# Attention scores of a hybrid decoder layer: one product over two key blocks in place of two

## Chip, core and metric

The kernel runs on one core of a Trainium2 chip. The metric is device time in microseconds (us): the median of three runs of the kernel before is 1100.19 us (1099.69 to 1100.69). The engines are named as the profile names them: PE (TensorE) with its weight loads PEld, DVE (VectorE), ACT (ScalarE), POOL (GpSimd) and SP (SyncE, which issues most DMAs).

## What is computed

One decoder layer over 1024 tokens of width 1024, in float32: an input projection, half of whose columns go to sliding-window attention with 8 query heads and 2 key heads of 64, the other half to a gated linear recurrence with four heads of 128; an output projection; and a squared-ReLU MLP of width 4096. What the change touches is the attention, in blocks of 128 queries, each against its own block of keys and the block ahead of it:

```python
def band(a):
    ab = a.reshape(B, nb, WINDOW, ATT_KV_HEADS, D)
    prev = jnp.pad(ab, ((0, 0), (1, 0), (0, 0), (0, 0), (0, 0)))[:, :-1]
    return jnp.concatenate([prev, ab], axis=2)

kk, vv = band(k), band(v)
s = jnp.einsum('bnqhgd,bnkhd->bnhgqk', qb, kk).astype(jnp.float32) * (D ** -0.5)
...
p = p / (jnp.sum(p, axis=-1, keepdims=True) + jnp.exp(sink - m))
o = jnp.einsum('bnhgqk,bnkhd->bnqhgd', p.astype(v.dtype), vv)
```

Here WINDOW is 128, so that there are 8 blocks, and D is 64.

## The kernel before, in words

The layer runs in stages on the one core: the modulation vectors and the first projections, attention (from about 84 to 188 us of the span), the recurrence heads, the output projection, and the MLP, which takes the last 600 us. Most products are split by hand into three float32r products of high and low parts (`proj3`); the attention works on plain float32, for which a product shows as two PE records, two passes.

`attention(tb)` (L523) is a generator for one block of 128 tokens, with two `yield`s inside. Its first part transposes the queries and keys of the block by PE (`pqT`, `pkT`), copies them out (`qT` by ACT, `kT` by DVE, L532 to L534) and forms the scores (L542 to L550): for two pairs of query columns (`mp`), two columns (`m`), the key block ahead and the own one (`src`), and two key heads (`g`) one product of 128 queries by 128 keys each. The key heads lie on partitions 0 to 63 and 64 to 127, so that the two products of a pair use different rows of the array. A block has 16 products, the first block 8. For each `mp`, `g` the scores of the key block ahead are copied out by ACT, and those of the own block go by a masked DVE copy into `comb` (L551 to L555). Maximum, exponentials with their sums (`sm`), the reciprocal `rd` and the scaling of `comb` follow (half on DVE, half on POOL). The second part, after the first `yield`, transposes the weights (`pT`), splits them by the mask into `pc` and `pp`, forms the output `oT`, its squares (`sqa`, ACT), their sum `sqr` (DVE), a transpose of that sum on PE (`ssp`), its sum `ssc`, two POOL operations (`t_att`, `r_att`) and a diagonal `dg`. The third part is one product `rb` (L611) with that diagonal and the scaling of the output (`q<-q,rb`).

The loop at L673 to L679 starts the parts of the 8 blocks against a row of fillers: the projections `pq`, `pk` of blocks 4 to 7, then eight `pv` products (`values`, 24 products of 512 columns each), one filler a step. Within that loop no engine's order is pinned (L640 takes the pins off): the framework's scheduler sets each engine's order from the dependences and its own estimate of times, and on the chip every engine then runs its list in that fixed order. So a filler product can stand between two steps of a block, and a changed instruction can move others. Buffers matter in two places: PSUM tiles of pool `pb` (five banks) hold `pqT`, `pkT`, the scores, `pT` and `oT`; `kT` has three buffers of 128 columns.

Of the kernel before, what the change touches and what calls it, by code (L numbers as in the profile page):

```python
# [9 lines left out]
F32 = mybir.dt.float32  # L10
F32R = mybir.dt.float32r
I32 = mybir.dt.int32
AF = mybir.ActivationFunctionType
# [3 lines left out]
P = 128  # L17
D = 1024
KB = D // P
TB = 8  # L20
# [27 lines left out]
def hybrid_layer(ctx: ExitStack, tc: tile.TileContext, I, out, dbg=None):  # L48
    nc = tc.nc
    ACT, DVE, POOL, PE, SP = (Queue(tc, e) for e in (nc.scalar, nc.vector, nc.gpsimd, nc.tensor, nc.sync))  # L50
# [35 lines left out]
    def t_(name, shape=(P, 512), dt=F32):  # L86
        return T2.tile(list(shape), dt, tag="t2", name=name)
# [4 lines left out]
    def tp_ps(name):  # L92
        return pb.tile([P, 512], F32, tag="b", name=name)
# [166 lines left out]
    XA = gactx.enter_context(tc.tile_pool(name="poolXA", bufs=1))  # L260
# [5 lines left out]
    for gate in range(2):  # L266
        gs = slice(64 * gate, 64 * gate + 64)
# [253 lines left out]
    kTs, vs = {}, {}  # L521

    def attention(tb):  # L523
# [4 lines left out]
        qT = t_(f"qT{tb}", [P, 4, P])  # L528
        ACT.activation(qT, pqT.rearrange("p (m t) -> p m t", m=4), AF.Copy)
        pkT = tp_ps(f"pkT{tb}")  # L530
        PE.transpose(pkT[:, :P], kv[:, 0:P], ident)
        kT = XA.tile([P, P], F32, tag="kT", bufs=3, name=f"kT{tb}")  # L532
        DVE.tensor_copy(kT, pkT[:, :P])
        kTs[tb] = kT  # L534
        aw = q
        a3 = aw.rearrange("p (m t) -> p m t", m=4)
        c5 = w_(f"comb{tb}", (P, 2, 2, 2, P))
# [4 lines left out]
        for mp in range(2):  # L542
            scs = [tp_ps(f"sc{tb}_{mp}_{g}").rearrange("p (m j) -> p m j", m=2) for g in range(2)]
            for m in range(2):
                for src in (tb - 1, tb) if tb else (tb,):
                    for g in range(2):
                        gs = slice(64 * g, 64 * g + 64)
                        js = slice(P, 2 * P) if src == tb else slice(0, P)
                        PE.matmul(scs[g][:, m, js], lhsT=qT[gs, 2 * mp + m, :], rhs=kTs[src][gs, :],
                                  start=True, stop=True)  # L550
            for g in range(2):  # L551
                sc = scs[g]
                if tb:
                    ACT.activation(c5[:, mp, g], sc[:, :, 0:P], AF.Copy)
                DVE.copy_predicated(c5[:, mp, g], mb, sc[:, :, P:2 * P])  # L555
# [33 lines left out]
        for g in range(2):  # L589
            vsl = slice(128 + 64 * g, 192 + 64 * g)  # L590
            og = o_ps[64 * g:64 * g + 64, :].rearrange("p (a x) -> p a x", a=2)
            if tb:
                PE.matmul(og, lhsT=kvn[tb - 1][:, vsl],
                          rhs=pp[:, :, 2 * g:2 * g + 2, :].rearrange("p a m q -> p a (m q)"), start=True, stop=False)
            PE.matmul(og, lhsT=kv[:, vsl], rhs=pc[:, :, 2 * g:2 * g + 2, :].rearrange("p a m q -> p a (m q)"),
                      start=(tb == 0), stop=True)
# [19 lines left out]
    def step(tb):  # L616
        if 0 <= tb < TB:
            next(att[tb])

    att = [attention(tb) for tb in range(TB)]  # L620
    for kb in range(2):
        qproj(kb)
# [962 lines left out]
    g = len(GROUPS) - 1  # L1585
# [3 lines left out]
    for step, (_, t, k) in enumerate(order):  # L1589
# [13 lines left out]
        if k >= 3 and t < 3:  # L1603
            tb = t + 4 * th
# [139 lines left out]
```

## Time and profile before

| what | value |
|---|---|
| median of three runs | 1100.19 us (1099.69 to 1100.69) |
| span of the profiled execution (first to last instruction) | 1097.6 us |
| time of that execution beside its span | not listed; the median lies 2.59 us above the span |
| PE busy | 1076.2 us, 98% of the span |
| DVE, ACT, POOL busy | 795.1, 584.6 and 373.2 us |
| chain that ended last | PE 92%, DVE 3%, ACT 1%, DMA 1%, POOL 1%, issue 1% |
| score products | 240 records, for 120 products |

A PE record of this profile begins where the product begins, but its end is modelled and lies after the beginning of the next one, so the time that a product takes from its engine is the distance from its start to the next start. A number in square brackets at a row's end is idle time of the engine ahead of it and who ended it; a record that is stretched while PE waits can hide such a wait.

### The profile page before, as it was taken

How to read it: one execution, taken by the hardware profiler on the slowest of the kernel's cores; microseconds unless marked ns; L12 is line 12 of the kernel's file. 1: busy time of each engine (PE TensorE's matmuls, PEld its weight loads, DVE VectorE, ACT ScalarE, POOL GpSimd, SP SyncE). 2: the span in 40 equal slices, each digit the busy share in tenths (PEclk: the TensorE clock that was granted, in tenths of full speed). 3: DMA queues.
4: the chain of work that ended last, by engine and by line, in shares of the span. 5: the costliest groups of instructions: out<-in, count | busy, mean ns of one | idle time of the engine just before them, and what ended most of it. 6: DMA issues, size and time to landing. Idle time of an engine off the chain costs nothing.

```text
span 1097.6 us, 16208 instructions
## 1 busy us (share of the span) xinstructions
PE 1076.2 (98%) x5547; PEld 878.2 (80%) x5547; DVE 795.1 (72%) x1323; ACT 584.6 (53%) x1206; POOL 373.2 (34%) x499
## 2 busy tenths in 40 slices
PE   8999999999999999999999999999999999999995
PEld 6788776778888888888888888888888888888884
DVE  4365777878865574559776767876767787899876
ACT  3445544364565764566655555556664543555434
POOL 1153211033324663432543444533333333310014
PEclk9999999999999999999999999999999999999998
DMA  9701301534310352324577676767998888998537
GB/s 347 265 7 57 117 1 43 181 101 140 125 56 11 108 182 96 125 79 144 194 246 249 233 259 227 257 216 244 320 364 289 275 299 259 337 308 272 169 76 131
DMA packets 101587, 203.37 MB, mean 185 GB/s; under 512 B 13025, under 2 KB 13681, under 8 KB 101505
## 3 DMA queue, kind: packets, MB, share of 16 engines
q1 hardware_dynamic: 85968, 154.52, 41.4%
q0 software_dynamic: 15392, 47.57, 14.3%
q8 instruction: 43, 0.70, 0.3%
q14 instruction: 40, 0.32, 0.1%
q10 hardware_dynamic: 144, 0.26, 0.1%
HBM read 147.25 MB, written 55.05 MB: 184 GB/s over the span
## 4 chain that ended last, share of the span: by engine, by line
PE 92%; DVE 3%; ACT 1%; DMA 1%; POOL 1%; issue 1%; SPq 0%; DVEq 0%; POOLq 0%; ACTq 0%
PE pda L39 16%; PE pua L39 14%; PE pdc L39 8%; PE po L39 8%; PE puc L39 7%; PE pu L39 4%; PE pdb L39 4%; PE pq L39 4%; PE phg L39 4%; PE phq L39 3%; PE pub L39 3%; PE phf L39 3%; PE pv L39 3%; PE pk L39 2%; PE o L39 1%; PE sc L39 1%
## 5 line engine op out<-in xcount | busy, mean ns | idle before, releaser
L39 POOL TENSOR_TENSOR b<-b,b 128x512 f32<-128x512 f32 x64 | 89.6, 1400 | 222.8 <-DMA b<-w_dn 222.4
L39 ACT ACTIVATE dw<-dwr 128x512 fp32r<-128x512 f32 x72 | 45.4, 630 | 46.5 <-DMA dwr<-td 32.4
L39 ACT ACTIVATE s<-s 128x512 f32<-128x512 f32 x84 | 53.0, 631 | 31.8 <-DVE s L39 30.5
L39 DVE TENSOR_TENSOR dw<-dwr,dw 128x512 fp32r<-128x512 f32 x72 | 53.6, 744 | 9.0 <-ACT dw L39 8.9
L39 DVE TENSOR_TENSOR acc<-pda,acc 128x512 f32<-128x512 f32 x68 | 46.5, 684 | 13.7 <-PE pda L39 13.3
L39 POOL DMA_DIRECT2D td<-b x64 | 36.3, 567 | 21.6 <-POOL b L39 18.7
L39 POOL TENSOR_TENSOR rrf<-ssf,mhalf 128x1 f32<-128x1 f32 x7 | 7.9, 1253 | 95.3 <-DVE ssf L39 95.3
L39 DVE TENSOR_TENSOR wt<-s,wt 128x512 fp32r<-128x512 f32 x42 | 37.2, 886 | 2.6 <-ACT wt L39 2.5
L39 ACT ACTIVATE s<-pua 128x512 f32<-128x512 f32 x28 | 16.7, 598 | 39.4 <-PE pua L39 33.9
L39 ACT ACT_TABLE_LOAD x28 | 35.9, 1283 | 1.2 <-PEq L1737 0.7
L39 DVE SCALAR_TENSOR_TENSOR macc<-wada,cs,macc 128x512 f32<-128x512 f32 x42 | 33.7, 803 | 3.4 <-DMA wada<-wada 2.9
L39 POOL DMA_DIRECT2D b<-w_dn x64 | 34.4, 540 | 0.0
L39 POOL TENSOR_TENSOR comb<-comb,rd 128x512 f32<-128x512 f32 x8 | 11.7, 1458 | 63.3 <-DVE rd L39 44.2
L39 PE MATMUL pua<-bt_0h,wt 128*128 128x512 f32 x84 | 32.7, 389 | 0.0
L39 PE MATMUL pua<-bt_1h,wt 128*128 128x512 f32 x84 | 32.7, 389 | 0.0
L39 PE MATMUL pua<-bt_3h,wt 128*128 128x512 f32 x84 | 32.7, 389 | 0.0
L39 PE MATMUL pua<-bt_2h,wt 128*128 128x512 f32 x84 | 32.7, 389 | 0.0
L39 DVE TENSOR_TENSOR wt<-a,wt 128x512 fp32r<-128x512 f32 x42 | 31.0, 738 | 0.9 <-ACT wt L39 0.9
L39 DVE TENSOR_TENSOR acc<-pdc,acc 128x512 f32<-128x512 f32 x36 | 24.6, 684 | 8.5 <-PE pdc L39 8.4
L39 ACT ACTIVATE wt<-s 128x512 fp32r<-128x512 f32 x42 | 26.3, 626 | 8.2 <-DVE s L39 8.0
L39 PE MATMUL pda<-dw,du_6h 128*128 128x512 f32 x96 | 29.6, 389 | 0.0
L39 PE MATMUL pda<-dw,du_7h 128*128 128x512 f32 x96 | 29.5, 389 | 0.0
(757 smaller groups left out, 3746.1 us busy)
## 6 DMA issues: line engine op xcount, KB each, us to landing
dur<-ud SPq DMA_DIRECT2D x112, 256.0 KB, 4.5
wada<-wada SPq DMA_DIRECT2D x64, 256.0 KB, 3.5
b<-w_dn POOLq DMA_DIRECT2D x64, 256.0 KB, 5.2
td<-b POOLq DMA_DIRECT2D x64, 256.0 KB, 3.3
dwr<-td SPq DMA_DIRECT2D x64, 256.0 KB, 4.3
a<-w_u SPq DMA_DIRECT2D x56, 256.0 KB, 4.4
dwr<-w_dn SPq DMA_DIRECT2D x48, 256.0 KB, 4.5
ud<-s SPq DMA_DIRECT2D x42, 256.0 KB, 3.6
```

The lines of the kernel that those rows point to most:

```text
L39: ins = op(*args, **kw)
```

## The change

The keys of a block and of the block ahead are put side by side in one tile of 2 x 128 columns. The transposed keys of block `tb` are copied out twice: by DVE into the second half of the block's own tile, and by ACT into the first half of the tile of block `tb + 1`. The scores of a (`mp`, `m`, `g`) are then one product of 256 columns, except in the first block, which has no keys ahead of it. The tile has two buffers in place of three.

```diff
         PE.transpose(pkT[:, :P], kv[:, 0:P], ident)
-        kT = XA.tile([P, P], F32, tag="kT", bufs=3, name=f"kT{tb}")
-        DVE.tensor_copy(kT, pkT[:, :P])
-        kTs[tb] = kT
+        if not tb:
+            kTs[0] = XA.tile([P, 2, P], F32, tag="kT", bufs=2, name="kT0")
+        kT = kTs[tb]
+        DVE.tensor_copy(kT[:, 1], pkT[:, :P])
+        if tb + 1 < TB:
+            kTs[tb + 1] = XA.tile([P, 2, P], F32, tag="kT", bufs=2, name=f"kT{tb + 1}")
+            ACT.activation(kTs[tb + 1][:, 0], pkT[:, :P], AF.Copy)
...
             for m in range(2):
-                for src in (tb - 1, tb) if tb else (tb,):
-                    for g in range(2):
-                        gs = slice(64 * g, 64 * g + 64)
-                        js = slice(P, 2 * P) if src == tb else slice(0, P)
-                        PE.matmul(scs[g][:, m, js], lhsT=qT[gs, 2 * mp + m, :], rhs=kTs[src][gs, :],
-                                  start=True, stop=True)
+                for g in range(2):
+                    gs, js = slice(64 * g, 64 * g + 64), slice(0 if tb else P, 2 * P)
+                    PE.matmul(scs[g][:, m, js], lhsT=qT[gs, 2 * mp + m, :],
+                              rhs=kT.rearrange("p a j -> p (a j)")[gs, js], start=True, stop=True)
```

The scheduler answers with another order. Three places show it. The first is PE in the score part of block 4 (blocks are counted from 0; the tiles' last numbers are buffer numbers). Before, the products with the keys of the block ahead (tile `kT_1460`) stand first, and then two `pv` products and `ssp` (of block 2):

```order
L39 MATMUL sc_0_0_1599<-kT_1460,qT_1592 128x128
L39 MATMUL sc_0_1_1600<-kT_1460,qT_1592 128x128
L39 MATMUL sc_1_0_1613<-kT_1460,qT_1592 128x128
L39 MATMUL sc_1_1_1614<-kT_1460,qT_1592 128x128
L39 MATMUL pv_1831<-whv4l,hhi_0_606 128x512
L39 MATMUL ssp_1577<-c_tab,sqr_1575 128x128
L39 MATMUL pv_1831<-whv4h,hlo_0_607 128x512
L39 MATMUL sc_0_0_1599<-kT_1596,qT_1592 128x128
L39 MATMUL sc_0_1_1600<-kT_1596,qT_1592 128x128
```

Ten more score products and `rb` follow there. Now:

```order
L39 MATMUL sc_0_0_1581<-kT_1449,qT_1573 128x256
L39 MATMUL sc_0_1_1582<-kT_1449,qT_1573 128x256
L39 MATMUL sc_0_0_1581<-kT_1449,qT_1573 128x256
L39 MATMUL sc_0_1_1582<-kT_1449,qT_1573 128x256
L39 MATMUL ssp_1558<-c_tab,sqr_1556 128x128
L39 MATMUL sc_1_0_1591<-kT_1449,qT_1573 128x256
L39 MATMUL sc_1_1_1592<-kT_1449,qT_1573 128x256
L39 MATMUL sc_1_0_1591<-kT_1449,qT_1573 128x256
L39 MATMUL sc_1_1_1592<-kT_1449,qT_1573 128x256
L39 MATMUL rb_1701<-dg_1566,ones 128x128
```

The two `pv` products are gone from the score part, and four score products in place of twelve stand between `ssp` and `rb`. Blocks 4 to 7 have this form in both kernels. Between the last `pT` of a block and the next `oT` there are 20 `pv` products, where the block of the rows below had 21; between `pkT` and the scores there are five, where it had three.

The second place is DVE from the end of the exponentials of block 3 to `ssc` of block 2 and the masked copies of block 4. Before:

```order
L39 TENSOR_TENSOR den_1510<-sm_1501,es_1499 128x8
L39 RECIPROCAL rd_1512<-den_1510 128x8
L39 TENSOR_TENSOR comb_1462<-comb_1462,rd_1512 128x512
L39 TENSOR_TENSOR q_864<-oT_1567,c_attw 128x512
L39 TENSOR_REDUCE sqr_1575<-sqa_1572 128x128
L39 COPY kT_1596<-pkT_1594 128x128
L39 TENSOR_REDUCE ssc_1579<-ssp_1577 128x1
L39 TENSOR_SCALAR dg_1585<-c_tab,r_att_1583 128x128
```

Now:

```order
L39 TENSOR_TENSOR den_1491<-sm_1482,es_1480 128x8
L39 COPY kT_1449<-pkT_1575 128x128
L39 RECIPROCAL rd_1493<-den_1491 128x8
L39 TENSOR_TENSOR q_864<-oT_1548,c_attw 128x512
L39 TENSOR_TENSOR comb_1451<-comb_1451,rd_1493 128x512
L39 TENSOR_REDUCE sqr_1556<-sqa_1553 128x128
L39 COPY_PREDICATED comb_1580<-c_mle,sc_0_0_1581 128x256
L39 TENSOR_REDUCE ssc_1560<-ssp_1558 128x1
L39 COPY_PREDICATED comb_1580<-c_mle,sc_0_1_1582 128x256
L39 TENSOR_SCALAR dg_1566<-c_tab,r_att_1564 128x128
```

The copy of the keys has moved from behind `sqr` to ahead of `rd`; the scaling of `comb` has moved behind `q<-oT`.

The third place is the SP queue behind the attention, where the modulation weights `wada_0_*` and the raw weights of the next head (`whf1r`, `whq1r`) are loaded. Before:

```order
L39 DMA whf1r_2602<-w_hd 128x512
L39 DMA wada_0_0_2370<-wada 128x512
L39 DMA wada_0_1_2373<-wada 128x512
L39 DMA wada_0_2_2376<-wada 128x512
L39 DMA wada_0_3_2379<-wada 128x512
L39 DMA wada_0_4_2382<-wada 128x512
L39 DMA whf1r_2606<-w_hd 128x512
L39 DMA wada_0_5_2385<-wada 128x512
```

Now:

```order
L39 DMA whf1r_2553<-w_hd 128x512
L39 DMA whf1r_2557<-w_hd 128x512
L39 DMA wada_0_0_2321<-wada 128x512
L39 DMA wada_0_1_2324<-wada 128x512
L39 DMA wada_0_2_2327<-wada 128x512
L39 DMA wada_0_3_2330<-wada 128x512
L39 DMA wada_0_4_2333<-wada 128x512
L39 DMA whq1r_2593<-w_hd 128x512
```

One load of a next head's weights has moved ahead of five modulation loads, and the next such load ahead of the other three.

## Rows read from the trace of the kernel before

**Rows 1.** The page: the chain that ended last, by engine.
```profile
PE 92%; DVE 3%; ACT 1%; DMA 1%; POOL 1%; issue 1%; SPq 0%; DVEq 0%; POOLq 0%; ACTq 0%
```

**Rows 2.** PE's timeline: start us, us, instruction, count [idle before <-releaser]. One attention period.
```profile
134.91 0.49 PE L39 MATMUL rb<-dg,ones 128*128 128x128 f32 x2
...
147.44 0.49 PE L39 MATMUL rb<-dg,ones 128*128 128x128 f32 x2
...
148.56 0.48 PE L39 MATMUL pv<-whv5h,hlo 128*128 128x512 f32 x1
...
153.54 1.09 PE L39 MATMUL oT<-pp,kv 128*64 128x512 f32 x4
...
155.91 0.27 PE L39 MATMUL pkT<-c_tab,kv 128*128 128x128 f32 x1
...
156.82 0.71 PE L39 MATMUL sc<-kT,qT 64*128 64x128 f32 x8
157.47 0.51 PE L39 MATMUL pv<-whv5h,hlo 128*128 128x512 f32 x1
157.95 0.33 PE L39 MATMUL ssp<-c_tab,sqr 128*128 128x128 f32 x1
...
158.44 1.61 PE L39 MATMUL sc<-kT,qT 64*128 64x128 f32 x24
159.97 0.49 PE L39 MATMUL rb<-dg,ones 128*128 128x128 f32 x2
```

**Rows 3.** PE's timeline at 18 and 22 us: float32 products of 32 weight columns.
```profile
17.96 1.08 PE L39 MATMUL pm<-wa,csr 128*32 128x128 f32 x32
...
22.18 1.07 PE L39 MATMUL pm<-wa,csr 128*32 128x256 f32 x16
```

**Rows 4.** DVE's timeline: from the exponentials' end to dg of one period.
```profile
142.67 0.17 DVE L39 TENSOR_TENSOR den<-sm,es 128x8 f32<-128x8 f32 x1 [2.15 <-ACT comb L39]
142.88 0.20 DVE L39 RECIPROCAL rd<-den 128x8 f32<-128x8 f32 x1
143.11 0.69 DVE L39 TENSOR_TENSOR comb<-comb,rd 128x512 f32<-128x512 f32 x1
143.72 0.68 DVE L39 TENSOR_TENSOR q<-oT,c_attw 128x512 f32<-128x512 f32 x1
144.32 1.04 DVE L39 TENSOR_REDUCE sqr<-sqa 128x128 f32<-128x512 f32 x1
145.28 0.28 DVE L39 COPY kT<-pkT 128x128 f32<-128x128 f32 x1
145.78 0.29 DVE L39 TENSOR_REDUCE ssc<-ssp 128x1 f32<-128x128 f32 x1 [0.22 <-PE ssp L39]
147.02 0.29 DVE L39 TENSOR_SCALAR dg<-c_tab,r_att 128x128 f32<-128x128 f32 x1 [0.94 <-POOL r_att L39]
```

**Rows 5.** PE's timeline where ssp starts in that period.
```profile
145.42 0.33 PE L39 MATMUL ssp<-c_tab,sqr 128*128 128x128 f32 x1
```

**Rows 6.** PE and DVE at the first block: the key transpose and its copy.
```profile
84.80 0.27 PE L39 MATMUL pkT<-c_tab,kv 128*128 128x128 f32 x1
...
85.11 0.29 DVE L39 COPY kT<-pkT 128x128 f32<-128x128 f32 x1 [5.29 <-PE pkT L39]
```

**Rows 7.** PE's timeline in block 3's score part.
```profile
119.96 0.33 PE L39 MATMUL ssp<-c_tab,sqr 128*128 128x128 f32 x1 [0.34 <-DVE sqr L39]
120.22 1.60 PE L39 MATMUL sc<-kT,qT 64*128 64x128 f32 x22
122.37 0.49 PE L39 MATMUL rb<-dg,ones 128*128 128x128 f32 x2 [0.55 <-DVE dg L39]
```

**Rows 8.** ACT's timeline: the first score copy of a period.
```profile
159.40 1.05 ACT L39 ACTIVATE comb<-sc 128x256 f32<-128x256 f32 x3 [2.64 <-PE sc L39]
```

**Rows 9.** PE's timeline behind the last scores.
```profile
183.27 1.06 PE L39 MATMUL pT<-c_tab,comb 128*128 128x128 f32 x8 [0.42 <-DVE comb L39]
```

**Rows 10.** Who waited for whom, PE over the whole span: us, times, longest.
```profile
PE phg L39 <- ACT f L39: 1.3, 1, 1.3
```

## The prediction

> **What bounds the kernel now.** Read the chain of waits first [rows 1]: 92% of the path to the last instruction is PE. A change off PE is therefore worth nothing unless PE comes to wait for it, and a change on PE is worth what it takes from PE's own list, as long as nothing else takes its place at the end. So read PE's timeline of the attention next. One period, from the `rb` of a block to the next `rb`, is 147.44 to 159.97 = 12.53 us [rows 2], with no idle time in the score part. There are four such periods (blocks 4 to 7). Then ask how near the other engines are to holding PE. Block 3 answers that: there PE already waits 0.34 us at `ssp` for DVE's `sqr`, and 0.55 us at `rb` for DVE's `dg` [rows 7]. Blocks 4 to 7 run the same parts and wait for neither, because `pv` fillers and sixteen score products stand ahead of these two instructions. The reader is to see that PE's order in the score part is balanced against a chain DVE - PE - DVE - POOL - DVE that is about as long as the fillers.
>
> **What 256 columns cost.** In the score part 24 records begin between 158.44 and 159.97 [rows 2]. They run as pairs, one on each half of the rows, so 12 steps take 1.53 us; with about 0.22 for the first step after another kind of product, a step is 0.11. The other eight records, 156.82 to 157.47, are 4 x 0.11 + 0.22 = 0.65 by the same rule. Is a step set by its 128 streamed columns or by something paid for each product? Rows 3 have the same float32 at either width: 32 records of 128 columns in 1.08 us and 16 records of 256 columns in 1.07 us. Half the products with double the columns take the same time, so the columns set it. A score part of 16 steps of 0.11 becomes 8 steps of 0.215: nothing is gained in the streaming (1.72 against 1.71 us).
>
> The Trainium skill, "TensorE: Matmul & The Clock Gate", section "LDWEIGHTS (loading the stationary operand)", has a load take P/1.2 ns where P is the number of weight columns, whatever the rows: an estimate of 107 ns for 128 columns. By that rule of the Trainium skill the step could be the load, the same whatever is streamed, and 256 columns could be free; no row of this kernel shows 256 columns behind a load of 128, and [rows 3], with 32 weight columns each, do not agree with a price per load.
>
> **PE's own list, one period.** From `rb` to the first `pv` 1.12 us; 21 `pv` from 148.56 to 153.54 are 0.237 each, so the 20 that now stand there are 4.74; `oT` to `pkT` 2.37 [rows 2]. `pkT` thus starts 8.23 after `rb`. From `pkT` to the scores is 0.91 with three `pv`, so 1.38 with five. The score part was 3.15 us (two runs of scores, two `pv`, `ssp`). Now there are two runs of four products each, 4 x 0.215 + 0.23 = 1.09, and `ssp` between them at 0.26 (119.96 to 120.22 [rows 7]), together 2.44. The sum is 8.23 + 1.38 + 2.44 = 12.05 against 12.53. Of the 0.48 less, 0.24 is a `pv` that has only gone elsewhere (-1 between `pT` and `oT`, +2 ahead of the scores, -2 in the score part); 0.24 is saved truly, one switch between `pv` and the scores less.
>
> **The chain beside it.** DVE's list of the period whose `rb` is at 134.91 [rows 2, 4] gives start distances: `rd` to `comb` 0.23, `comb` to `q` 0.61, `q` to `sqr` 0.60, `sqr` 1.04 long. Before, `kT` stood behind `sqr`, so `rd` and all that follows waited only for `den`, at 142.67 - 134.91 = 7.76 after `rb`. Now the copy of the keys stands ahead of `rd`, and DVE runs its list in order, so `rd`, `q`, `comb`, `sqr` all wait for PE's `pkT`. `pkT` at 8.23, the copy 0.31 behind it (84.80 to 85.11 [rows 6]), at 8.54. `den` has 0.78 to spare against that, so it is not last even if it comes somewhat later. Then 0.20 (copy) + 0.12 (`rd`, a little shorter than its row) + 0.60 (`q`) + 0.61 (`comb`) + 1.04 (`sqr`) + 0.06 (to PE): `ssp` can start 11.17 after `rb`. Before, it started at 145.42 - 134.91 = 10.51 [rows 5]. From `ssp` to `ssc` 0.36 [rows 4, 5], `ssc` to `dg` 1.24, `dg` 0.29, to PE 0.06: 1.95. So the next `rb` can start 13.12 after the last one, not 12.05.
>
> PE would reach `ssp` at 8.23 + 1.38 + 1.09 = 10.70 and wait 0.47 there; behind `ssp` it has 0.26 + 1.09 = 1.35 us of scores where the chain takes 1.95, and waits 0.60 at `rb`. Behind these two stand only scores and the next block's `pT`: a wait there is a wait for all of PE. The twelve products and a `pv` that covered this before are now four.
>
> **The sum**, against the span of 1097.6 us, which lies 2.59 under the median of 1100.19:
> - Four periods of 13.12 - 12.53 = 0.59: **+2.36**.
> - Four `pv` less done by the last `rb` of these periods, to be run later, 4 x 0.237: **+0.95**.
> - Blocks 2 and 3 wait for the chain already [rows 7] and get the same copy. Bounds 0 (their order of DVE is only half moved) and 2 x 0.59 = 1.2; I take **+0.5**, in the middle.
> - Behind the last scores PE waits 0.42 for `comb` [rows 9]. `pv` left over can fill that: bounds -0.9 (all four are hidden) and 0; I take **-0.4**, that wait.
> - ACT's seven extra copies of keys, 0.3 us each by DVE's row [rows 6], stand behind `qT` and ahead of the score copies, where ACT idles 2.64 us waiting for `sc` [rows 8]: **0**. Without that idle time they would cost 7 x 0.3 = 2.1.
> - The loads on the SP queue: half of one head's raw weights comes five loads earlier, part of the next three earlier, the modulation loads later. The one row of the next head's products that waits is `phg` for ACT's `f`, 1.3 us [rows 10]. Bounds -1.3 (gone) and +1.3 (as much again); no row says which: **0**.
> - Two `kT` buffers of double width: the tile of a block is first written in the block ahead of it, after the scores of the block two before have long been read: **0**.
>
> Together 2.36 + 0.95 + 0.5 - 0.4 = 3.4: 1097.6 + 3.4 = 1101.0 for the span, and with the same 2.59 around it **1103.6 us**. With the bounds of the terms the forecast's own range is 1102.0 to 1105.0.
>
> **Rivals.**
> A. *The chain is shorter than its rows, and PE's own list decides* (ends on the other side, not slower). If `den`, `q` and `sqr` come sooner when DVE is not held by `comb`, PE runs at its own 12.05 with 0.24 saved per period: 4 x 0.24 = -1.0, 1099.2 us. It decides where the path from `rb` over `pkT` and the copy to the next `rb` is under 12.05, so 1.07 us shorter than I add up. For it: the `pv` fillers make `pkT` itself movable, and each row is from one period. Against it: block 3 shows the same chain already ahead of PE [rows 7], and every piece of the sum is a duration of an engine that had nothing else to do. In between (a chain of 12.5) lies about 1101.
>
> B. *The loads' new order holds the next head*. The wait of `phg` [rows 10] grows by as much as it is, on top of the forecast: 1103.6 + 1.3 = 1104.9. For it: eight modulation loads have gone behind parts of two heads' weights. Against it: PE reaches `phg` later by 3 us, which gives the loads that much more.
>
> C. *A score step is not its columns* but a price per product, so that 256 columns take the 0.11 of 128. Then each block saves 8 steps of 0.11 = 0.9 us, seven blocks 6.2. Alone it shows nothing, since PE would only wait longer for the chain; with A it gives 1099.2 - 6.2 = 1093.0. For it: no row has 256 columns against 128 weight columns. Against it: the steps of [rows 3]. The Trainium skill's rule on weight loads (same page and section) is such a price.
>
> **How the numbers follow.** About 0.2%, 2.2 us, is what a measurement of this kernel can tell from no change: faster is below 1098.0, slower above 1102.4. The forecast has 0.64 (nearly all of it above 1102.4), A with its in-between values 0.22 (mostly same), B 0.09 (slower), C 0.05 (faster). So slower 0.72, same 0.21, faster 0.07. The range takes in the forecast's own range, most of B and A's value nearly: 1099.4 to 1105.8; out of it lie C, A's lower half and a chain longer than I think, some 0.2.
>
> **What would show it.** In the profile after: score records of 256 columns, pairs 0.215 apart (0.11 would be C); in blocks 4 to 7 `ssp` with about 0.5 of idle time ended by DVE's `sqr`, and `rb` with about 0.6 ended by `dg`, and `rb` to `rb` 13.1 us (12.0 without such waits would be A); on DVE a wait of the copy `kT` for `pkT` ahead of `rd`; `phg` waiting 1.3 us for `f` once (2.6 would be B). I am wrong if the four periods come out at 12.5 or less, or if time appears behind 190 us, where I put none.

## The result, and the profile after

The changed kernel takes 1105.02 us (median; 1102.88 to 1108.49), the kernel before 1099.94 in the same comparison: a ratio of 1.0049, 95% interval 1.0037 to 1.0061. A second set of runs of the same kernel gave 1104.22 us and a ratio of 1.0038, 1.0024 to 1.0052. It is slower by 4 to 5 us, as forecast; 1103.6 had been predicted.

The page of the changed kernel, its span and the chain that ended last, by engine:

```profile
span 1104.5 us, 16000 instructions
...
PE 86%; DVE 6%; DMA 3%; issue 1%; ACT 1%; POOL 1%; SPq 0%; DVEq 0%; POOLq 0%; ACTq 0%
```

PE's share of the path fell from 92% [rows 1] to 86%, and DVE's doubled (89% and 5% in a second profile, experiment 7). The waits of PE over the whole span (us, times, longest) say where DVE came in:

```profile
PE ssp L39 <- DVE sqr L39: 4.0, 5, 1.0
PE rb L39 <- DVE dg L39: 3.9, 7, 0.8
...
PE phg L39 <- ACT f L39: 1.3, 1, 1.3
```

In the kernel before, the first two were:

```profile
PE rb L39 <- DVE dg L39: 1.6, 4, 0.6
...
PE ssp L39 <- DVE sqr L39: 0.6, 2, 0.3
```

PE's timeline of the attention, to be held against [rows 2]:

```profile
151.28 0.49 PE L39 MATMUL rb<-dg,ones 128*128 128x128 f32 x2 [0.55 <-DVE dg L39]
...
159.50 0.27 PE L39 MATMUL pkT<-c_tab,kv 128*128 128x128 f32 x1
...
160.86 1.13 PE L39 MATMUL sc<-kT,qT 64*128 64x256 f32 x8
162.96 0.33 PE L39 MATMUL ssp<-c_tab,sqr 128*128 128x128 f32 x1 [0.97 <-DVE sqr L39]
163.22 1.13 PE L39 MATMUL sc<-kT,qT 64*128 64x256 f32 x8
164.90 0.49 PE L39 MATMUL rb<-dg,ones 128*128 128x128 f32 x2 [0.55 <-DVE dg L39]
```

Both waits are there, ended by the instructions that were forecast; the period is 164.90 - 151.28 = 13.62 us where 13.12 was expected and 12.53 stood before. DVE's timeline of that period answers to [rows 4], and POOL's has one line that matters:

```profile
159.32 0.17 DVE L39 TENSOR_TENSOR den<-sm,es 128x8 f32<-128x8 f32 x1 [2.74 <-ACT comb L39]
159.81 0.29 DVE L39 COPY kT<-pkT 128x128 f32<-128x128 f32 x1 [0.33 <-PE pkT L39]
...
160.13 0.64 DVE L39 TENSOR_TENSOR q<-oT,c_attw 128x512 f32<-128x512 f32 x1
160.69 1.29 DVE L39 TENSOR_TENSOR comb<-comb,rd 128x512 f32<-128x512 f32 x1
161.90 1.01 DVE L39 TENSOR_REDUCE sqr<-sqa 128x128 f32<-128x512 f32 x1
...
163.33 0.29 DVE L39 TENSOR_REDUCE ssc<-ssp 128x1 f32<-128x128 f32 x1
...
164.56 0.29 DVE L39 TENSOR_SCALAR dg<-c_tab,r_att 128x128 f32<-128x128 f32 x1 [0.59 <-POOL r_att L39]
```

```profile
160.38 1.04 POOL L39 TENSOR_TENSOR comb<-comb,rd 128x512 f32<-128x512 f32 x1 [9.48 <-ACT qT L39]
```

`comb` takes 1.29 us on DVE (1.21 to the next start) where it took 0.69 (0.61) before. All the rest of the chain came as added up.

One period of this profile, 136.04 to 151.28, is 15.24 us, because a stretch of some 3 us behind its `rb` ran at a granted clock of 0.50 (1.2 GHz). The windows there (PE, PEld, DVE, ACT, POOL busy with counts, granted clock, DMA share, GB/s):

```profile
132.00:136.50 4.50, 2.98 (x22) 1.97 (x22) 3.72 (x7) 1.32 (x4) 1.30 (x3) 1.00 0.00 0
136.50:139.00 2.50, 2.50 (x12) 2.31 (x11) 2.43 (x4) 0.00 (x0) 0.00 (x0) 0.50 0.03 7
```

In the 4.5 us ahead of the fall PE was busy for only 2.98. The changed kernel's second profile, experiment 7, has the same waits and no such stretch, so the accounting is made on that one.

### The profile page after: what moved, and what is told of

It reads as the page before. It is cut to its first block, busy times and chain, and to the rows that moved or that the text cites. A ratio compares the mean times of both kernels' runs of the same rounds, so it can differ in the third digit from the quotient of the medians.

```text
span 1104.5 us, 16000 instructions
## 1 busy us (share of the span) xinstructions
PE 1077.6 (98%) x5435; PEld 876.5 (79%) x5435; DVE 793.6 (72%) x1323; ACT 585.9 (53%) x1213; POOL 370.7 (34%) x499
## 4 chain that ended last, share of the span: by engine, by line
PE 86%; DVE 6%; DMA 3%; issue 1%; ACT 1%; POOL 1%; SPq 0%; DVEq 0%; POOLq 0%; ACTq 0%
PE pua L39 14%; PE pda L39 14%; PE po L39 8%; PE puc L39 7%; PE pdc L39 6%; PE pu L39 4%; PE pdb L39 4%; PE pq L39 4%; PE phg L39 3%; PE pub L39 3%; PE phf L39 3%; PE phq L39 3%; PE pv L39 3%; PE pk L39 2%; PE o L39 1%
## 5 line engine op out<-in xcount | busy, mean ns | idle before, releaser
L39 DVE TENSOR_TENSOR wt<-a,wt 128x512 fp32r<-128x512 f32 x42 | 35.1, 836 | 0.9 <-ACT wt L39 0.9
L39 DVE TENSOR_TENSOR s<-puc,s 128x512 f32<-128x512 f32 x14 | 9.7, 691 | 30.8 <-issue 28.3
L39 PE MATMUL pdc<-dw,du_3h 128*128 128x512 f32 x96 | 29.6, 389 | 0.0
```

Of the source, the lines that this page charges most:

```text
L39: ins = op(*args, **kw)
```

## The experiments

**1. The tile and the copies without the wide products.**

```diff
-                for g in range(2):
-                    gs, js = slice(64 * g, 64 * g + 64), slice(0 if tb else P, 2 * P)
-                    PE.matmul(scs[g][:, m, js], lhsT=qT[gs, 2 * mp + m, :],
-                              rhs=kT.rearrange("p a j -> p (a j)")[gs, js], start=True, stop=True)
+                for a, g in [(a, g) for a in ((0, 1) if tb else (1,)) for g in range(2)]:
+                    gs = slice(64 * g, 64 * g + 64)
+                    if True:
+                        PE.matmul(scs[g][:, m, a * P:a * P + P], lhsT=qT[gs, 2 * mp + m, :],
+                                  rhs=kT[gs, a, :], start=True, stop=True)
```

> The changed kernel's tile and its two copies of the keys (DVE and ACT) are kept, but each score product of 256 columns is again two of 128. The scheduler then gives PE and DVE the order of the kernel before (21 pv ahead of oT, 3 pv ahead of the scores, sc x4, pv, ssp, pv, sc x12, rb; the copy kT behind sqr). Theory O (the order costs the time: DVE's copy of kT ahead of rd, scores without pv around ssp): no ssp or rb wait in blocks 4 to 7, rb to rb 12.53 us, time 1099.9 +- 1, as before. Rival T (the doubled copies or the two buffers of the tile cost it): 1102 to 1105, with ACT's or DVE's copies ending PE's waits. Rival W (the products of 256 columns cost it by themselves): also as before, so this run alone does not part O from W.

Measured: 1099.83 us against 1099.83, ratio 0.9996 (0.9986 to 1.0005). `rb` to `rb` is 12.54 us, and PE's waits are those of before (us, times, longest):

```profile
PE rb L39 <- DVE dg L39: 1.6, 4, 0.5
...
PE ssp L39 <- DVE sqr L39: 0.6, 2, 0.3
```

So the seven extra copies on ACT and the tile cost nothing. What costs comes with the width: the products themselves, or the order that the scheduler gives for them.

**2. `sqr` ahead of `comb` and `q`.** The products stay 256 wide, and one order is set on DVE (`mark` holds an instruction that was noted before, and `issue_after` puts what follows behind it):

```diff
-        DVE.tensor_tensor(a3, o_ps.rearrange("p (m t) -> p m t", m=4), attw..., ALU.mult)
+        with nullcontext() if tb + 1 >= TB else tc.issue_after(mark["comb", 0, tb + 1].ins):
+            DVE.tensor_tensor(a3, o_ps.rearrange("p (m t) -> p m t", m=4), attw..., ALU.mult)
```

> The changed kernel with one more order on DVE: the product q<-oT of a block stands behind the scaling of comb of the next block. The scheduler's answer on DVE is kT, rd, sqr, comb, q (in the changed kernel kT, rd, q, comb, sqr); on PE still 20 pv ahead of oT and 5 ahead of the scores, and then one score product, ssp, seven score products, rb. The copy kT stays ahead of rd, the products stay 256 columns wide. Theory O: sqr starts at 8.86 after rb and ssp can start at 9.96 where PE comes to it at about 10.0; from ssp the chain takes 1.95 and PE has 0.26 + 7 x 0.215 + 0.23 = 2.0 of its own. Both waits go below 0.15 us, the period falls from 13.64 to 12.1, and the time to 1105.0 - 4 x 1.5 = 1099 (1098 to 1100.5), with no stretch at the lower granted clock in the attention. Theory W (256 columns cost by themselves): still 1103 or more. If only the ssp wait goes, 1101 to 1102.

Measured: 1100.76 us, ratio 1.0002 (0.9992 to 1.0012). Some four of the lost microseconds are back with 256 columns in place; the expected 1099 was missed, and PE's and DVE's timelines show why:

```profile
135.42 0.49 PE L39 MATMUL rb<-dg,ones 128*128 128x128 f32 x2 [0.33 <-DVE dg L39]
...
145.62 0.33 PE L39 MATMUL ssp<-c_tab,sqr 128*128 128x128 f32 x1
...
148.20 0.49 PE L39 MATMUL rb<-dg,ones 128*128 128x128 f32 x2 [0.33 <-DVE dg L39]
```

```profile
144.27 1.06 DVE L39 TENSOR_REDUCE sqr<-sqa 128x128 f32<-128x512 f32 x1
145.25 0.86 DVE L39 TENSOR_TENSOR comb<-comb,rd 128x512 f32<-128x512 f32 x1
146.04 0.68 DVE L39 TENSOR_TENSOR q<-oT,c_attw 128x512 f32<-128x512 f32 x1
146.64 0.28 DVE L39 TENSOR_REDUCE ssc<-ssp 128x1 f32<-128x128 f32 x1
```

The wait at `ssp` is gone, as expected. But `comb` and `q` now stand between `sqr` and `ssc`, so that `ssc` starts 1.02 after `ssp` in place of 0.36. The chain from `ssp` to `rb` is 2.58, the period 12.78, and 0.33 of waiting remains. The expectation had moved `sqr` and forgotten what it was moved past.

**3. The copy of the keys back behind `sqr`.**

```diff
-        DVE.tensor_copy(kT[:, 1], pkT[:, :P])
+        with nullcontext() if tb < 2 else tc.issue_after(mark["sqr", tb - 2].ins):
+            DVE.tensor_copy(kT[:, 1], pkT[:, :P])
```

> The changed kernel with the copy kT of a block put back behind sqr of the block two before it. The scheduler then puts DVE as in the kernel before (rd, comb, q, sqr, kT) and on PE 20 pv ahead of oT, 11 pv ahead of ssp, and pv and all eight score products between ssp and rb. Theory O: nothing on DVE waits for pkT ahead of sqr, ssp can start 10.5 after rb and PE comes to it at about 11; between ssp and rb PE has 2.7 us of work where the chain takes 1.95. No wait at ssp or rb in blocks 4 to 7, DVE's comb 0.69 us again and POOL's 1.45. The period is longer (13.8 us) but holds 32 pv in place of 25, so that is work and not loss: 1098 to 1099.5. Theory W: 1103 or more. If the scores now wait for the late copy of kT (PE waiting for DVE's kT), 1100 to 1102.

Measured: 1106.03 us, ratio 1.0047 (1.0031 to 1.0062): a clear miss, 7 us above what was expected. The time lies where theory W put it, but not for its reason. In blocks 4 to 7 all is nearly as foreseen: period 13.62 with 32 `pv` in it, no wait at `rb`, 0.2 at `ssp`, and DVE's `comb` is 0.69 again. The price comes behind them, in PE's waits over the span and in its windows at 195 us:

```profile
PE phq L39 <- ACT whq0h L39: 4.1, 1, 4.1
...
PE phq L39 <- DVE whq0l L39: 1.3, 1, 1.3
```

```profile
195.00:200.00 5.00, 0.73 (x2) 0.30 (x2) 5.00 (x9) 1.78 (x4) 0.00 (x0) 0.89 0.66 195
200.00:205.00 5.00, 4.99 (x12) 2.61 (x14) 3.53 (x6) 0.00 (x0) 0.00 (x0) 0.50 0.33 114
```

The 192 `pv` products are a stock. This order spends seven more of it in each block than the changed kernel, comes to the next head's `phf` at 195.16 (197.90 in the kernel before) and asks for that head's weights before they are split: 4.1 + 1.3 us of waiting, and the granted clock at 0.50 in the 5 us behind the longer of them.

**4. POOL's half of the scaling on DVE, behind `dg`.**

```diff
         for mp in range(2):
             ch = c[:, 4 * mp:4 * mp + 4, :]
-            (POOL if mp else DVE).tensor_tensor(
-                ch, ch, rd..., ALU.mult)
-        yield
+            if mp:
+                yield
+            with tc.issue_after(mark["ssc", tb - 1].ins) if mp and tb else nullcontext():
+                DVE.tensor_tensor(ch, ch, rd..., ALU.mult)
```

> The changed kernel with POOL's half of the scaling of comb done by DVE instead, behind dg of the block ahead; DVE's list up to sqr (kT, rd, q, comb, sqr) and PE's list of blocks 4 to 7 (20 pv, oT, 5 pv, sc x4, ssp, sc x4, rb) stay as in the changed kernel. It tests the term that came out larger than predicted: DVE's scaling of comb took 1.29 us in the changed kernel where POOL's half began 0.3 us ahead of it, and 0.69 in the kernel before where POOL's began 0.14 behind it. Theory P (the two engines hold each other up, and the one that comes second pays): DVE's comb is 0.69 again, sqr is 0.6 sooner, the ssp wait falls from about 1.0 to 0.4, the period from 13.64 to about 13.1, the time by 4 x 0.55 = 2.2 to about 1102.8, less if oT comes to wait for pp (DVE has 0.6 more behind dg). Rival S (its length comes from what stands around it on DVE): comb stays 1.29, time 1105 or more.

Measured: 1101.61 us, ratio 1.0010 (1.0000 to 1.0020). DVE's and PE's timelines:

```profile
146.44 0.68 DVE L39 TENSOR_TENSOR comb<-comb,rd 128x512 f32<-128x512 f32 x1
```

```profile
150.10 0.49 PE L39 MATMUL rb<-dg,ones 128*128 128x128 f32 x2 [0.59 <-DVE dg L39]
...
161.20 0.33 PE L39 MATMUL ssp<-c_tab,sqr 128*128 128x128 f32 x1 [0.37 <-DVE sqr L39]
...
163.19 0.49 PE L39 MATMUL rb<-dg,ones 128*128 128x128 f32 x2 [0.59 <-DVE dg L39]
```

With POOL's half gone and DVE's and PE's lists the same up to `sqr`, `comb` is 0.68 again and the period 163.19 - 150.10 = 13.09 us: the 13.12 of the prediction's sum. The two periods beside it are as long; the first of the four takes 14.27, where PE waits, among others, 0.63 for the half of `comb` that DVE now scales later. Theory P holds: DVE's longer `comb` was POOL's work beside it. The time itself lies 1.2 us below the expected 1102.8 and does not measure `comb` alone; `phg`, for one, waits 0.2 for `f` here.

**5. `q` behind `ssc`.** With 256 columns; the version that the second run pointed to.

```diff
-        DVE.tensor_tensor(a3, o_ps.rearrange("p (m t) -> p m t", m=4), attw..., ALU.mult)
...
-        DVE.tensor_reduce(ssc, ssp[:, 0:P], AX.X, ALU.add)
+        with tc.issue_after(DVE.tensor_reduce(ssc, ssp[:, 0:P], AX.X, ALU.add).ins):
+            DVE.tensor_tensor(a3, o_ps.rearrange("p (m t) -> p m t", m=4), attw..., ALU.mult)
```

> The changed kernel (products of 256 columns) with the product q<-oT behind ssc on DVE. The scheduler's answer on DVE is kT, rd, sqr, comb, ssc, q, dg; on PE 20 pv, oT, 5 pv, one score product, ssp, seven score products, rb. In the run with sqr ahead of comb and q, rb still waited 0.33 us in each block, because comb and q stood between sqr and ssc (ssp to rb 2.58 us). Theory O (DVE's order was the whole loss): ssc now follows comb at once, q fits into the 0.95 us in which DVE waits for POOL's r_att, ssp to rb falls to PE's own 2.25, the period from 12.78 to 12.45, the time by some 6 x 0.33 = 2 us below that run's: 1098.8 (1098 to 1099.8), about 0.1% below the kernel before. Theory W (256 columns cost by themselves): no lower than that run, 1100.5 or more.

Measured: 1097.01 us, ratio 0.9972 (0.9961 to 0.9983): faster than both kernels, and lower than was expected. DVE's timeline, and PE's:

```profile
155.87 1.02 DVE L39 TENSOR_REDUCE sqr<-sqa 128x128 f32<-128x512 f32 x1
156.81 0.90 DVE L39 TENSOR_TENSOR comb<-comb,rd 128x512 f32<-128x512 f32 x1
157.63 0.28 DVE L39 TENSOR_REDUCE ssc<-ssp 128x1 f32<-128x128 f32 x1
157.83 0.68 DVE L39 TENSOR_TENSOR q<-oT,c_attw 128x512 f32<-128x512 f32 x1
158.86 0.29 DVE L39 TENSOR_SCALAR dg<-c_tab,r_att 128x128 f32<-128x128 f32 x1 [0.35 <-POOL r_att L39]
```

```profile
147.03 0.49 PE L39 MATMUL rb<-dg,ones 128*128 128x128 f32 x2
...
156.59 0.70 PE L39 MATMUL sc<-kT,qT 64*128 64x256 f32 x2
157.22 0.33 PE L39 MATMUL ssp<-c_tab,sqr 128*128 128x128 f32 x1
157.48 1.99 PE L39 MATMUL sc<-kT,qT 64*128 64x256 f32 x14
159.40 0.49 PE L39 MATMUL rb<-dg,ones 128*128 128x128 f32 x2
```

No wait is shown at `ssp` or `rb` in blocks 4 to 7: `rb` to `rb` is 12.37 us (12.88 in the first of the four), 2.18 from `ssp` to `rb`. `q` fills time in which DVE waited for POOL anyway. The edit names one instruction; the scheduler's answer moved `sqr` ahead of `comb` and three score products behind `ssp` as well.

PE's own list has grown all the same. In the changed kernel it is 13.62 less the two waits of 0.97 and 0.55, so 12.10, near the 12.05 of the prediction. The 0.27 more lies in the scores: one product ahead of `ssp` and seven behind it take 0.63 + 1.92 us to the next start, where four and four take 1.13 + 1.13 without the waits. That the lone product has no partner on the other half of the rows is the likely reason; no run tests it.

**6. The same with 128 columns.** The product loop of the first experiment, the edit of the fifth.

> The same with two products of 128 columns in place of each of 256 (tile and copies as in the changed kernel). It is the pair to the run before it: the order on DVE up to rb is freed in both, so the difference is the width alone, and the few pv that the scheduler places otherwise (21 and 3 in place of 20 and 5; two score products, ssp, fourteen). Theory E (a step is its columns, 256 cost twice 128): the two runs agree within 0.1% (1.1 us), pairs of scores 0.107 us apart here and 0.215 there. Rival C (256 columns cheaper than two of 128): this one is slower by up to 6 us. Rival W: this one is faster by 1 us or more.

Measured: 1097.40 us, ratio 0.9976 (0.9967 to 0.9985). The two intervals lie on each other; 0.4 us is less than the runs can tell apart. The score rows behind `ssp`:

```profile
157.41 1.93 PE L39 MATMUL sc<-kT,qT 64*128 64x128 f32 x28
```

28 records of 128 columns take 1.93 us, 14 of 256 take 1.99. Theory E fits: neither width is ahead by more than the runs can tell. The pair is less clean than the expectation has it, because the scheduler's order differs in more than the `pv`. Here DVE has `rd`, `comb`, `sqr`, `kT`, `ssc`, `q`, with `comb` at 0.69 us; in the fifth `kT` stands ahead of `rd`, and `comb`, behind `sqr`, takes 0.90. That a score step costs its columns at either width rests on the score rows.

**7. The changed kernel once more.**

> The changed kernel itself once more, for a second profile and more runs. In the first profile one stretch of 3.2 us behind the rb at 136.04 ran at the lower granted clock (0.50) and made that period 15.24 us in place of 13.64. If that is part of each execution, a period of over 15 us and a mean clock of 0.994 come back, and the time is 1105 +- 0.5. If it comes in some executions only, the four periods are 13.64 us here, the mean clock is 0.996, the span is lower by 1.6 us for it, and the time lies between 1102.9 and 1105, with the executions of lower clock the longer ones.

Measured: 1104.22 us, ratio 1.0038 (1.0024 to 1.0052). PE's timeline:

```profile
122.37 0.49 PE L39 MATMUL rb<-dg,ones 128*128 128x128 f32 x2 [0.82 <-DVE dg L39]
...
135.97 0.49 PE L39 MATMUL rb<-dg,ones 128*128 128x128 f32 x2 [0.55 <-DVE dg L39]
...
176.90 0.49 PE L39 MATMUL rb<-dg,ones 128*128 128x128 f32 x2 [0.55 <-DVE dg L39]
```

The periods are 13.60 to 13.66 us, and the clock is at full speed between 132 and 142 us, although PE is busy for the same 2.98 of the 4.5 us between 132 and 136.5. The stretch at 1.2 GHz is not part of each execution. Whether it makes the longer ones is less clear: in the first six runs the spans are 1101.1 and 1102.6 us at a mean clock of 0.996, and 1104.5 and 1106.7 at 0.994; but this profile's execution has 0.995 where 0.996 was expected, and with 1101.8 us it is the shortest of its five.

**8. `q` late and the copy of the keys back.** The edits of the third and the fifth together.

> As the run with q behind ssc, and the copy kT put back behind sqr as well. The scheduler answers with eight pv ahead of ssp, and one pv and all eight score products between ssp and rb, 29 pv in a period. Theory F (pv are a fixed stock of 192, and what is put ahead into one place is missing later): the attention blocks have no PE wait, but the stock ends ahead of the last two blocks' rb and the next head's products start before their weights are split; the run that put kT back alone waited 4.1 and 1.3 us for these weights. With 28 to 29 pv in place of 32 per period that shortage is smaller: 1099 to 1102, slower than the run with q late by 0.5 us or more. Rival: no shortage, 1097.5 to 1098.5, the fastest of all.

Measured: 1099.50 us, ratio 0.9996 (0.9987 to 1.0004), slower than the fifth by 2.5 us, as theory F has it. Its waits, though, are less a shortage of weights than others (us, times, longest):

```profile
PE ssp L39 <- DVE sqr L39: 2.3, 5, 1.2
PE rb L39 <- DVE dg L39: 1.7, 3, 1.2
...
PE phg L39 <- ACT whg0h L39: 0.5, 1, 0.5
```

Most of it stands in the first blocks (1.2 at the `ssp` of block 1, 1.2 at the first `rb`). So the time came as expected, and the mechanism only in part.

## Why the prediction was right, and where it was off

- *Streaming and the tile.* Right. Two runs of eight records took 1.13 us each at 256 columns and 0.71 at 128 [rows 2]: four steps, 0.42 more, 0.105 a step. Rival C, and the load rule of the Trainium skill ("TensorE: Matmul & The Clock Gate", section "LDWEIGHTS (loading the stationary operand)") as an explanation of the step, fall with these rows, and with experiments 5 and 6. The load records of the scores take 0.18 to 0.19 us at either width, against the 0.107 estimated by that rule of the Trainium skill; the measurement decides. The copies on ACT cost nothing (experiment 1).
- *The chain.* Right in its place and its links. After the `rb` at 151.28 `pkT` came at 8.22 (8.23 in the sum), the copy at 8.53 (8.54), `q` at 8.85 (8.86), `comb` at 9.41 (9.46). From `ssp` to `rb` it took 1.94 (1.95), and `rb` waited 0.55 (0.60).
- *The step that was off* is the term "0.61 (`comb`)", taken from [rows 4]. It measured 1.21, so `ssp` started at 11.68 and not 11.17, and waited 0.97 and not 0.47. Four periods make 4 x (13.63 - 12.53) = +4.4 where +2.36 stood. The row priced `comb` as DVE's alone, and the prediction took every piece of the sum for an engine's that "had nothing else to do"; but POOL scales the other half of the same tile beside it. The trace of before shows the price in the last block, which the prediction does not use; POOL's timeline there and in the period of [rows 4], and DVE's:

```profile
143.25 1.45 POOL L39 TENSOR_TENSOR comb<-comb,rd 128x512 f32<-128x512 f32 x1 [8.80 <-DVE rd L39]
...
181.17 1.41 POOL L39 TENSOR_TENSOR comb<-comb,rd 128x512 f32<-128x512 f32 x1 [9.12 <-DVE rd L39]
```

```profile
181.59 1.53 DVE L39 TENSOR_TENSOR comb<-comb,rd 128x512 f32<-128x512 f32 x1
```

  At 143 us DVE starts first (143.11), keeps its 0.69, and POOL pays: 1.45 where it takes 1.04 in the changed kernel. At 181 us POOL's stands first and DVE pays: 1.53 (POOL's own 1.41 there begins while DVE is at another product, `macc`, until 181.59). The change moved `comb` behind `q`, and so from first to second. The Trainium skill, "SBUF — State Buffer", section "SBUF: two separate sides", has it that DVE and GpSimd (POOL) share one port pair, held as a lock for a whole instruction when DVE reads two operands from SBUF and GpSimd reads SBUF too (as both do here), and that the later one waits it out. The rows agree in size: in the changed kernel POOL ends at 160.38 + 1.04 = 161.42, and 0.61 behind that is 162.03, where DVE's next instruction began at 161.90. Experiment 4 shows that POOL's half is the cause by taking it away, and experiment 3 by putting `comb` first again; that it is the port through which the two meet is the Trainium skill's account, which no run here tests by itself.
- *The smaller terms*, from the second profile of the changed kernel. Blocks 2 and 3: the `rb` at 122.37 stands where it stood, though the attention began 0.23 earlier, so +0.2 (+0.5 expected). Behind the last period the next head's `phf` starts 0.3 later still (+0.95 - 0.4 = +0.55 expected). `phg` waited 0.8 in place of 1.3, so -0.5 (0 expected); rival B did not occur. With the 0.23 of the start the sum is 4.4 + 0.2 + 0.3 - 0.5 - 0.2 = 4.2, the 1101.8 - 1097.6 of the spans. These terms were put at +1.05 and came out at -0.2, so they gave back 1.25 of the +2.0 of `comb`. That 1103.6 came as close as it did is luck to that extent. The range of 1102.0 to 1105.0 that the prediction calls the forecast's own does not follow from its bounds either: they add up to 1102.6 to 1104.7 without the loads, and to 1101.3 to 1106.0 with them.
- *Rival A* (PE's own list decides) did not occur in the changed kernel, but experiment 5 is its case: with DVE out of the way PE ran its own list, 12.37 a period and not the 12.05 that was added up for four products on either side of `ssp`.
- *Not foreseen*: a stretch at 1.2 GHz behind two of the waits, to which the first profile lost 1.6 us. That the waits brought it is not shown, since the same waits stand elsewhere without it.

What stays open: how far the gain of experiments 5 and 6 could be had in the kernel before without the new tile. Experiments 1 and 6 together make it likely, since tile and copies cost nothing there; it was not run by itself.

## What to carry to other kernels

Here a step was set by its columns, and the wider product was worth nothing by itself: look in the trace for the same type at two widths before counting on a wider one. Where a scheduler sets the order, an edit is first of all a new order; compare the lists on the waiting engine and the one that it waits for, and ask of each moved instruction what it now stands behind. In this kernel one instruction moved on DVE (`q` behind `ssc`, into a wait that was there anyway), with the order that the scheduler gave in answer, was worth more than the width on either side: 1097.0 us against 1099.9 and 1105.0.

## What the runs showed of the hardware that was not expected

- The same 128 x 512 scaling took 0.68 to 0.69 us on DVE alone or when it began ahead of POOL's half, 1.28 to 1.53 when it began some 0.3 to 0.4 us behind it. POOL's half took 1.04 us, and 1.40 to 1.49 where DVE was already at this scaling or at another product of two tiles (`macc`). With `sqr` ahead of it DVE's took 0.78 to 0.90: POOL was 0.7 to 0.8 us into its own.
- PE's granted clock fell to 0.50 behind 4.1 us of waiting (experiment 3), and once behind a stretch of two waits of 0.97 and 0.55 us (first profile of the changed kernel), while the same two waits, four times in a row, left it at 1.00 in the second profile.
